# Recurrent heads: the product of decayed keys moved to VectorE alone, in two parts

## The chip, the cores and the metric

The kernel runs on one core of a Trainium2 chip. The metric is device time in microseconds, from the first to the last instruction of one launch with what little lies around it; the median of several runs is taken. Smaller is better.

## The reference: what is computed

One decoder layer on 1024 tokens of width 1024. After an RMS norm, one wide projection feeds two groups of heads: four differential softmax heads and four gated linear attention ("recurrent") heads. Their outputs are normalised, concatenated, projected back and added to the input; a SwiGLU feed-forward block follows. The change lies in the recurrent heads, whose core within a chunk is

```
b = jnp.cumsum(gi, axis=-2)                      # gi: log forget gates, <= 0
diff = b[:, :, :, None, :] - b[:, :, None, :, :]
decay = jnp.exp(jnp.where(causal, diff, -jnp.inf))
A = jnp.einsum('bhtk,bhsk,bhtsk->bhts', qi, ki, decay)
o_intra = jnp.einsum('bhts,bhsv->bhtv', A, vi)
```

The decay differs for each pair of tokens and each key channel, so A is not one plain matrix product.

## The kernel before

**Tiling and stages.** The wide projection runs in eight blocks of columns, each over eight tiles of 128 tokens, as three TensorE products of split float32 operands (function `mm3`, lines 259 to 261). The heads' own work is cut into tasks that a planner (`Order`) places between the steps of the projection by estimated costs and due times, so TensorE always has projection products (`pp`) between those of the heads. Tile then sets the order of the instructions on each engine with its own model, so instructions of different tasks interleave, and it gives each engine's queue its waits. Later come the output projection and the feed-forward block, from about 430 us on; they are not touched.

**The recurrent heads.** They are worked in pairs (class `GlaPair`), and each pair in two halves of 512 tokens. So there are four stretches of this work, starting near 143, 189, 315 and 361 us. In each half there are four windows i = 0 to 3 of 128 tokens. For a window, `factors` (line 618) builds two tiles of seven levels each: X (decayed keys, 128 partitions by 7 x 128) and Q (decayed queries, the same size). A level lv splits the window into blocks of 2^lv tokens and takes the decay of each token against the last token of its neighbouring block:

- differences of the cumulated gates into X: lines 632 and 633, levels 0 to 2 by POOL (GpSimd), levels 3 to 6 by DVE (VectorE);
- one exponential over all of X by ACT (line 634);
- seven products by DVE, one for each level, that write Q from one half of X and the queries (line 638);
- the product of X with the keys kT in place (line 643), levels 0 and 1 by POOL, levels 2 to 6 by DVE. A level of X may be overwritten only after its Q has been read from it.

Then `intra` (line 647) makes the seven products of Q and X on TensorE (line 656), four levels into one PSUM bank and three into another, and DVE copies the masked parts into the tile `at` (line 661, seven instructions). `outputs` (line 665) multiplies `at` with the values (line 673, tile `pgo`). X and Q have two buffers each, so the differences for window i + 2 wait until the products of window i have read X. The banks for the products and for `pgo` come from one ring of two (tag `ms`), so line 673 of window 0 needs a bank from which the four copies of line 661 of window 1 have read.

Of the kernel before, what the change touches and what calls it, by code (L numbers as in the profile page):

```python
# [18 lines left out]
P = 128  # L19
# [9 lines left out]
NLEV = 7  # L29
# [19 lines left out]
def _block_cols(kind, i):  # L49
    if kind == "D":  # L50
        c = [(128 * i, 128), (512 + 128 * i, 128), (1024 + 128 * i, 128)]
        if i == 0:
            c.append((3072, 16))
        return c
    if kind == "A":
        return [(1536 + 128 * i, 128), (1792 + 128 * i, 128), (2048 + 256 * i, 128)]
    return [(2048 + 256 * i + 128, 128), (2560 + 256 * i, 256)]


BLOCK_COLS = [_block_cols(*b) for b in BLOCKS]  # L60
NIN = len(BLOCKS)

OUT_COLS = [(0, 384), (384, 384), (768, 256)]
BLOCK_N = [sum(n for _, n in c) for c in BLOCK_COLS] + [n for _, n in OUT_COLS]
# [94 lines left out]
def decoder_layer(ctx: ExitStack, tc, xt, vecs, lams, w_proj, w_up, w_gu, w_dn, out):  # L159
    nc = tc.nc  # L160
# [92 lines left out]
    def split_scaled(src, gain, hi, lo):  # L253

        nc.scalar.activation(hi, src, AF.Copy, scale=gain)  # L255
        nc.vector.scalar_tensor_tensor(lo, src, gain, hi.bitcast(F32), ALU.mult, ALU.subtract)  # L256
# [44 lines left out]
    def split_unit(b, d, raw):  # L301
# [3 lines left out]
        l = wp.tile([P, n], F32R, name=f"wl{b}_{d}", tag="wl", bufs=9)  # L305
        if b < NIN:
            split_scaled(raw, vec[:, 8 + d : 9 + d], h, l)
# [215 lines left out]
    class GlaPair:  # L523
# [94 lines left out]
        def factors(self, hf, i):  # L618

            p = self.p  # L620


            X = gp.tile([P, NLEV, P], F32, name=f"X{p}_{hf}_{i}", tag="X", bufs=2)
            Q = gp.tile([P, NLEV, 2, 64], F32, name=f"Q{p}_{hf}_{i}", tag="Q", bufs=2)
            o = slice(P * i, P * i + P)
            v4 = lambda a, c: a.rearrange("p (n h c) -> p n h c", h=2, c=c)
            for lv in range(NLEV):
                c = 1 << lv
                xv, bv = v4(X[:, lv, :], c), v4(self.bT[:, o], c)
                ref = bv[:, :, 0, c - 1 : c].to_broadcast([P, 64 // c, c])  # L630
                eng = nc.gpsimd if lv < 3 else nc.vector
                eng.tensor_sub(xv[:, :, 0, :], ref, bv[:, :, 0, :])
                eng.tensor_sub(xv[:, :, 1, :], bv[:, :, 1, :], ref)
            nc.scalar.activation(X, X, AF.Exp)
            for lv in range(NLEV):
                c = 1 << lv
                xv = v4(X[:, lv, :], c)
                nc.vector.tensor_mul(
                    Q[:, lv].rearrange("p g (n c) -> p g n c", c=c),
                    xv[:, :, 1, :].unsqueeze(1).to_broadcast([P, 2, 64 // c, c]),  # L640
                    self.qT[:, :, o].rearrange("p g (n h c) -> p g n h c", h=2, c=c)[:, :, :, 1, :])
            for eng, lvs in ((nc.gpsimd, slice(0, 2)), (nc.vector, slice(2, NLEV))):
                eng.tensor_mul(X[:, lvs], X[:, lvs],  # L643
                               self.kT[:, o].unsqueeze(1).to_broadcast([P, lvs.stop - lvs.start, P]))
            self.XQ[i] = (X, Q)

        def intra(self, hf, i):

            p, (X, Q) = self.p, self.XQ.pop(i)
            at = gp.tile([P, 2, P], F32, name=f"at{p}_{hf}_{i}", tag="at", bufs=3)  # L650
            for hh in range(2):
                nc.scalar.mul(at[:, hh, :], ident8, self.dg[:, 2 * i + hh : 2 * i + hh + 1])
            for lvs in ((0, 1, 2, 3), (4, 5, 6)):
                pa = psum.tile([P, 4, 2, 64], F32, name=f"pa{p}_{hf}_{i}_{lvs[0]}", tag="ms")
                for k, lv in enumerate(lvs):
                    nc.tensor.matmul(pa[:, k], X[:, lv, :], Q[:, lv], start=True, stop=True)  # L656
                for k, lv in enumerate(lvs):
                    c = 1 << lv
                    ov = at.rearrange("p g (n h c) -> p g n h c", h=2, c=c)[:, :, :, 1, :]
                    mv = masks[:, lv, :].rearrange("p (n c) -> p n c", c=c).bitcast(I32)  # L660
                    nc.vector.copy_predicated(ov, mv.unsqueeze(1).to_broadcast([P, 2, 64 // c, c]),
                                              pa[:, k].rearrange("p g (n c) -> p g n c", c=c))
            self.at[hf, i] = at
# [207 lines left out]
    def open_gla():  # L871
        nonlocal gp, gqT, states
        xctx.close()
        gp = gctx.enter_context(pool("gp"))
        states = [gp.tile([P, 256], F32, name=f"S{k}") for k in range(2)]

        gqT = gp.tile([P, 2, 512], F32, name="gqT")
        for S in states + [gqT]:
            nc.gpsimd.memset(S, 0.0)

    for b, (kind, i) in enumerate(BLOCKS):
        obj = heads[i] if kind == "D" else pairs[i]
        evac = obj.evac if kind == "D" else (obj.evac_b if kind == "B" else obj.evac_a)
        for t in range(NT):
# [8 lines left out]
            if b == 0 and t == NT - 1:  # L893
                open_gla()
            if b == NIN - 1 and t % 4 == 3:
                if t == 7:
# [77 lines left out]
    for k, (o, n) in enumerate(OUT_COLS):  # L974
        b = NIN + k
        left = list(range(ND)) if k + 1 < len(OUT_COLS) else []
        for hf in range(2):
# [9 lines left out]
            for cc in range(n // P):  # L987
                c, w = o // P + cc, slice(P * cc, P * cc + P)
# [5 lines left out]
                h = hs[hf][c]  # L994
# [142 lines left out]
    for pr in range(NJ // 2):  # L1137
# [3 lines left out]
        X = [psum.tile([P, 512], F32, name=f"X{pr}_{m}", tag=("mm", "ms")[pr % 2]) for m in range(2)]  # L1141
# [292 lines left out]
```

## Time and profile before

| what | value |
|---|---|
| median of 3 runs | 1241.39 us (1240.34 to 1243.83) |
| the profiled execution, whole | 1245.05 us |
| its span, first to last instruction | 1243.3 us |
| TensorE (PE) busy | 1203.3 us, 97% of the span |
| VectorE (DVE) busy | 878.2 us, 71% |
| ScalarE (ACT) busy | 574.5 us, 46% |
| GpSimd (POOL) busy | 279.9 us, 23% |
| mean granted TensorE clock | 0.993 |

PE is busy nearly throughout, so time can come only from its few stops and from the stretches at a lower granted clock. The busy shares are averages over stages with different limits: what matters is which engine ends last in front of each stop.

### The profile page before, as it was taken

Reading aid. Unit: us, or ns where it says so; the run is one execution under the profiler, and the core shown is the slowest. Engines: PE = TensorE matmul, PEld = TensorE weight load, DVE = VectorE, ACT = ScalarE, POOL = GpSimd, SP = SyncE. Lnnn points to the kernel's source line nnn. Section 1 sums busy time; section 2 is a strip of 40 time slices with the busy share of each in tenths; the row PEclk is TensorE's granted clock in tenths of the full one; section 3 lists DMA queues with packets and bytes.
Section 4 is the critical chain, followed back from the end, with each engine's and each line's share of the span. In section 5 each row is a group of like instructions: output and inputs, shape, how many; then the busy total and the mean of one; then the engine's idle time right before and its main releaser. Section 6 shows DMA issues by size and latency. Waiting matters only on the chain.

```text
span 1243.3 us, 17114 instructions
## 1 busy us (share of the span) xinstructions
PE 1203.3 (97%) x6068; PEld 1012.7 (81%) x6068; DVE 878.2 (71%) x1804; ACT 574.5 (46%) x1171; POOL 279.9 (23%) x282
## 2 busy tenths in 40 slices
PE   7899998999889999999989999999999999999998
PEld 6789888889878978788768888888888888888787
DVE  6864489854888777546997666866677656677885
ACT  5656354555543676534643333333333335444432
POOL 4700314000431000000053434534354330000000
PEclk9999999999999999999999999999999999999999
DMA  6101010102100633221023231322223277743351
GB/s 212 39 28 44 17 52 18 52 26 60 39 31 19 175 96 119 85 93 67 2 102 136 85 114 73 127 94 102 100 87 127 84 254 295 264 153 94 94 178 69
DMA packets 57656, 121.41 MB, mean 98 GB/s; under 512 B 5969, under 2 KB 25570, under 8 KB 53346
## 3 DMA queue, kind: packets, MB, share of 16 engines
q1 hardware_dynamic: 57570, 120.31, 28.5%
q8 instruction: 48, 0.79, 0.3%
q14 instruction: 38, 0.31, 0.1%
HBM read 88.04 MB, written 32.24 MB: 97 GB/s over the span
## 4 chain that ended last, share of the span: by engine, by line
PE 84%; DVE 8%; ACT 3%; DMA 2%; POOL 1%; issue 1%; SPq 0%; DVEq 0%; ACTq 0%; POOLq 0%
PE X L261 6%; PE X L259 6%; PE X L260 6%; PE pp L259 6%; PE pp L261 5%; PE pp L260 5%; PE Z L261 3%; PE Z L260 3%; PE Z L259 3%; PE s L417 3%; PE po L461 3%; PE V L259 2%; PE V L260 2%; PE V L261 2%; PE po L259 2%; PE po L261 2%
## 5 line engine op out<-in xcount | busy, mean ns | idle before, releaser
L259 PE MATMUL pp<-wh,nh 128*128 128x384 f32 (+1 forms) x512 | 186.6, 365 | 9.0 <-ACT wh L255 5.8
L261 PE MATMUL pp<-wh,nl 128*128 128x384 f32 (+1 forms) x512 | 178.1, 348 | 0.0
L260 PE MATMUL pp<-wl,nh 128*128 128x384 f32 (+1 forms) x512 | 178.0, 348 | 0.0
L259 PEld LDWEIGHTS pp<-wh,nh 128*128 128x128 f32 x512 | 99.0, 193 | 19.4 <-ACT wh L255 6.4
L261 PEld LDWEIGHTS pp<-wh,nl 128*128 128x128 f32 x512 | 98.4, 192 | 2.2 <-issue 2.0
L260 PEld LDWEIGHTS pp<-wl,nh 128*128 128x128 f32 x512 | 98.7, 193 | 1.7 <-DVE wl L256 0.8
L1174 POOL TENSOR_TENSOR ac<-ac,gt 128x512 f32<-128x512 f32 x30 | 46.4, 1547 | 161.5 <-DVE ac L1159 153.5
L1080 POOL TENSOR_TENSOR S1f<-fr 128x512 f32<-128x512 f32 x20 | 27.0, 1351 | 246.6 <-DVE ndist L951 238.4
L1171 ACT ACTIVATE gt<-gt 128x512 f32<-128x512 f32 x40 | 25.3, 633 | 112.3 <-DVE gt L1170 59.5
L430 ACT ACTIVATE e<-e,nm 128x128 f32<-128x128 f32 (+7 forms) x64 | 49.3, 771 | 32.9 <-DVE nm L422 32.8
L259 PE MATMUL po<-mh,wh 128*128 128x512 f32 x128 | 51.2, 401 | 0.0
L261 PE MATMUL po<-mh,wl 128*128 128x512 f32 x128 | 50.6, 395 | 0.0
L260 PE MATMUL po<-ml,wh 128*128 128x512 f32 x128 | 50.4, 394 | 0.0
L256 DVE SCALAR_TENSOR_TENSOR wl<-wr,vec,wh 128x384 fp32r<-128x384 f32 (+1 forms) x64 | 40.5, 659 | 9.5 <-ACT wh L255 9.4
L1080 POOL TENSOR_TENSOR S4f<-fr,S2f 128x512 f32<-128x512 f32 x20 | 33.7, 1687 | 53.8 <-DVE ucl L251 51.7
L251 DVE TENSOR_TENSOR ufl<-S3f,ufh 128x512 fp32r<-128x512 f32 x22 | 15.2, 690 | 39.0 <-ACT ufh L250 39.0
L1172 DVE TENSOR_TENSOR gt<-gt,ndist 128x512 f32<-128x512 f32 x40 | 31.6, 790 | 15.8 <-ACT gt L1171 14.0
L461 PE MATMUL po<-v,wT 128*128 128x128 f32 x288 | 39.9, 283 | 2.0 <-ACT wT L451 2.0
L557 POOL TENSOR_TENSOR go<-go,gs 128x1024 f32<-128x1024 f32 x4 | 10.2, 2539 | 140.1 <-ACT gs L556 140.1
L422 DVE CUSTOM_DVE_ANT_0 e<-s,ndist 128x512 f32<-128x512 f32 (+3 forms) x64 | 36.7, 586 | 7.0 <-PE s L417 6.2
L255 ACT ACTIVATE wh<-wr,vec 128x384 fp32r<-128x384 f32 (+1 forms) x64 | 37.5, 615 | 8.8 <-DMA wr<-in_w_proj 7.0
L656 PE MATMUL pa<-Q,X 128*128 128x128 f32 x224 | 32.3, 291 | 9.3 <-POOL X L643 9.2
(555 smaller groups left out, 3535.8 us busy)
## 6 DMA issues: line engine op xcount, KB each, us to landing
fr<-in_w_gu SPq DMA_DIRECT2D x22, 1024.0 KB, 4.9
A<-act SPq DMA_DIRECT2D x77, 256.0 KB, 3.1
wr<-in_w_proj SPq DMA_DIRECT2D x72, 192.0 KB, 2.4
act<-ac SPq DMA_DIRECT2D x11, 1024.0 KB, 3.9
B<-in_w_dn SPq DMA_DIRECT2D x44, 256.0 KB, 5.4
act<-sm SPq DMA_DIRECT2D x11, 768.0 KB, 4.9
h<-in_xt SPq DMA_DIRECT2D x16, 256.0 KB, 5.1
hd<-h SPq DMA_DIRECT2D x16, 256.0 KB, 2.0
```

What stands on the lines that cost most here:

```text
L255: nc.scalar.activation(hi, src, AF.Copy, scale=gain)
L256: nc.vector.scalar_tensor_tensor(lo, src, gain, hi.bitcast(F32), ALU.mult, ALU.subtract)
L259: nc.tensor.matmul(ps, ah, bh, start=first, stop=False, **k)
L260: nc.tensor.matmul(ps, ah, bl, start=False, stop=False, **k)
L261: nc.tensor.matmul(ps, al, bh, start=False, stop=last, **k)
L417: nc.tensor.matmul(ps[m][:, :n], self.qk["q", hq][a][r, P * iq : P * iq + P], self.qk["k", ch][b][r, :n], start=(j == 0), stop=(j == 2))
L422: nc.vector.tensor_tensor_reduce(e[m][:, 512 * ch : 512 * ch + n], ps[m][:, :n], ndist[:, o : o + n], scale=-slope, scalar=nm[:, m, 0:1] i ...
L430: nc.scalar.activation(e[m][:, :cols], e[m][:, :cols], AF.Exp, bias=nm[:, m, nch - 1 : nch], scale=-1.0, accum_out=l[:, m : m + 1])
L461: nc.tensor.matmul(po[:, 0:P], self.wT[i, g][:, P * k : P * k + P], self.v[g][:, k, :], start=(kb == 0), stop=(kb == i))
L656: nc.tensor.matmul(pa[:, k], X[:, lv, :], Q[:, lv], start=True, stop=True)
L1080: (eng.tensor_sub if op == "-" else eng.tensor_add)(r, a, b)
L1174: nc.gpsimd.tensor_mul(quarter(q), quarter(q), g)
```

## The change

The Q products and the key products are done in two parts that follow the two PSUM banks: levels 0 to 3, then levels 4 to 6. In each part DVE makes the Q products of its levels and then one key product over all its levels. POOL no longer takes part in the key product; it keeps the differences of levels 0 to 2. `intra` uses the same table of levels and is otherwise unchanged.

```
+LEVELS = ((0, 1, 2, 3), (4, 5, 6))
...
-            for lv in range(NLEV):
-                c = 1 << lv
-                xv = v4(X[:, lv, :], c)
-                nc.vector.tensor_mul(
-                    Q[:, lv].rearrange("p g (n c) -> p g n c", c=c),
-                    xv[:, :, 1, :].unsqueeze(1).to_broadcast([P, 2, 64 // c, c]),
-                    self.qT[:, :, o].rearrange("p g (n h c) -> p g n h c", h=2, c=c)[:, :, :, 1, :])
-            for eng, lvs in ((nc.gpsimd, slice(0, 2)), (nc.vector, slice(2, NLEV))):
-                eng.tensor_mul(X[:, lvs], X[:, lvs],
-                               self.kT[:, o].unsqueeze(1).to_broadcast([P, lvs.stop - lvs.start, P]))
+            for lvs in LEVELS:
+                for lv in lvs:
+                    c = 1 << lv
+                    xv = v4(X[:, lv, :], c)
+                    nc.vector.tensor_mul(
+                        Q[:, lv].rearrange("p g (n c) -> p g n c", c=c),
+                        xv[:, :, 1, :].unsqueeze(1).to_broadcast([P, 2, 64 // c, c]),
+                        self.qT[:, :, o].rearrange("p g (n h c) -> p g n h c", h=2, c=c)[:, :, :, 1, :])
+                r = slice(lvs[0], lvs[-1] + 1)
+                nc.vector.tensor_mul(X[:, r], X[:, r], self.kT[:, o].unsqueeze(1).to_broadcast([P, len(lvs), P]))
```

## Rows read from the trace of the kernel before

**Rows 1.** The page: busy time, share and instructions of each engine.

```profile
PE 1203.3 (97%) x6068; PEld 1012.7 (81%) x6068; DVE 878.2 (71%) x1804; ACT 574.5 (46%) x1171; POOL 279.9 (23%) x282
```

**Rows 2.** Who waited for whom, PE, 140 to 410 us: total, times, longest.

```profile
PE pa L656 <- POOL X L643: 9.2, 4, 2.8
PE pp L259 <- DVE gv L544: 2.1, 4, 0.6
PE pgo L673 <- DVE at L661: 2.0, 2, 1.0
PE pgo L673 <- DVE X L633: 2.0, 2, 1.0
```

**Rows 3.** Timeline of PE, first and second stretch: start, length, [idle before <- releaser].

```profile
153.36 1.83 PE L656 MATMUL pa<-Q,X 128*128 128x128 f32 x14 [1.78 <-POOL X L643]
...
164.58 0.68 PE L673 MATMUL pgo<-gv,at 128*128 128x128 f32 x4 [1.01 <-DVE X L633]
...
199.46 2.24 PE L656 MATMUL pa<-Q,X 128*128 128x128 f32 x14 [2.82 <-POOL X L643]
...
212.82 0.68 PE L673 MATMUL pgo<-gv,at 128*128 128x128 f32 x4 [1.03 <-DVE at L661]
```

**Rows 4.** Instructions of line 643: count, ns min/median/max, first and last start.

```profile
L643 POOL TENSOR_TENSOR X<-X,gkT x16: 770/1302/3600, 149.7 to 388.9; 128x256 f32<-128x256 f32 x16
L643 DVE TENSOR_TENSOR X<-X,gkT x16: 808/834/1104, 150.7 to 390.0; 128x640 f32<-128x640 f32 x16
```

**Rows 5.** Timeline of POOL, first stretch.

```profile
149.71 4.86 POOL L643 TENSOR_TENSOR X<-X,gkT 128x256 f32<-128x256 f32 x2 [1.70 <-DVE Q L638]
```

**Rows 6.** Timeline of DVE, first stretch (149 to 165 us).

```profile
149.08 1.69 DVE L638 TENSOR_TENSOR Q<-X,gqT 128x128 f32<-128x128 f32 x8
150.70 0.81 DVE L643 TENSOR_TENSOR X<-X,gkT 128x640 f32<-128x640 f32 x1
151.43 1.29 DVE L638 TENSOR_TENSOR Q<-X,gqT 128x128 f32<-128x128 f32 x6
...
152.91 1.08 DVE L643 TENSOR_TENSOR X<-X,gkT 128x640 f32<-128x640 f32 x1
154.56 0.44 DVE L661 COPY_PREDICATED at<-masks,pa 128x128 f32<-128x128 int32 x1 [0.57 <-PE pa L656]
155.29 0.23 DVE L632 TENSOR_TENSOR X<-bT 128x64 f32<-128x64 f32 x1 [0.30 <-PE pa L656]
...
164.16 0.28 DVE L661 COPY_PREDICATED at<-masks,pa 128x128 f32<-128x128 int32 x1
```

**Rows 7.** Timeline of DVE, second stretch.

```profile
195.19 1.69 DVE L638 TENSOR_TENSOR Q<-X,gqT 128x128 f32<-128x128 f32 x8
...
207.30 0.45 DVE L661 COPY_PREDICATED at<-masks,pa 128x128 f32<-128x128 int32 x1 [1.37 <-PE pa L656]
...
209.41 0.23 DVE L632 TENSOR_TENSOR X<-bT 128x64 f32<-128x64 f32 x1 [1.18 <-PE pa L656]
...
211.13 1.14 DVE L638 TENSOR_TENSOR Q<-X,gqT 128x128 f32<-128x128 f32 x2
```

**Rows 8.** Busy time of all engines by stretch, with granted clock (PEclk) and DMA.

```profile
core 0: us, PE busy (x) PEld busy (x) DVE busy (x) ACT busy (x) POOL busy (x), PEclk, DMA share, GB/s
143.00:168.00 25.00, 21.52 (x139) 20.15 (x138) 23.59 (x85) 11.04 (x20) 13.90 (x27) 1.00 0.12 38
188.00:213.00 25.00, 21.12 (x128) 19.99 (x128) 22.11 (x76) 9.36 (x16) 14.18 (x27) 0.93 0.06 22
```

**Rows 9.** PE alone: stretch, length, busy (instructions), granted clock, DMA share, GB/s.

```profile
153.36:156.42 3.06, 3.06 (x22) 1.00 0.01 3
199.46:204.06 4.60, 4.60 (x22) 0.64 0.00 0
...
443.07:446.49 3.42, 3.42 (x16) 0.50 0.42 116
```

**Rows 10.** Timeline of PE near 443 us.

```profile
442.98 1.38 PE L461 MATMUL po<-v,wT 128*128 128x128 f32 x5 [2.00 <-ACT wT L451]
```

More of the change, by code (lines that the diff above doesn't have):

```diff
@@ L652, in intra @@
                 nc.scalar.mul(at[:, hh, :], ident8, self.dg[:, 2 * i + hh : 2 * i + hh + 1])
-            for lvs in ((0, 1, 2, 3), (4, 5, 6)):
+            for lvs in LEVELS:
                 pa = psum.tile([P, 4, 2, 64], F32, name=f"pa{p}_{hf}_{i}_{lvs[0]}", tag="ms")
```

## The prediction

> **What bounds the kernel now.** I read the page first: PE is busy for 97% of the span, DVE for 71%, POOL for 23% [rows 1]. So only PE's stops can be won, and with them time at a lower clock. Next the waits of PE between 140 and 410 us, where the recurrent heads run: it stopped four times, 9.2 us in all, with the products of line 656 waiting for POOL's part of line 643; four times, about 1.0 us each, at line 673 for DVE; and four times, 2.1 us in all, for line 544 on DVE [rows 2]. The timeline shows one long stop in each stretch, at its first window: 1.78 us in the first, 2.82 in the second [rows 3]. The third repeats the first and the fourth the second: (9.2 - 1.78 - 2.82) / 2 is 2.3, the mean of such a pair.
>
> Why POOL is late: its piece of line 643 takes 770 ns at best and 3600 at worst [rows 4]. In the first stretch it begins at 149.71 and two pieces hold it for 4.86 us [rows 5], while DVE runs Q products and its own key product without a gap [rows 6]. POOL's op is slow because it runs beside DVE's.
>
> The trace also prices the long stop's second effect. [...] So each long stop costs 1.5 us more, twice: 3.1 us. Stops and clock together, 9.2 + 3.1 = 12.3 us, are the most that the change can win here.
>
> Last, what else is tight. DVE is busy for 23.59 of 25 us in the first stretch and 22.11 of 25 in the second [rows 8]. That is nearer its limit than the 71% suggests.
>
> **Part by part.** *Removed: 16 POOL pieces.* Behind them on POOL stand only the differences of later windows, which wait for a free buffer of X anyway. What they take from DVE goes too. A DVE key product takes 0.81 us alone and 1.08 beside POOL's [rows 6], a relief of 0.27 for window 1 of each stretch. The two Q products from 211.13 take 1.14 us [rows 7] where one costs 0.20 (eight in 1.62, from 149.08 to 150.70 [rows 6]); POOL's key piece began beside them, and I put 0.5 of the excess down to it, once in each stretch. The late windows of the second and fourth have up to 1.10 [rows 4].
>
> [...]
>
> *Added: key products on DVE.* 640 columns occupy DVE from 150.70 to 151.43, 0.73 us, and 128 columns 0.20 [rows 6], so 1.04 ns a column. 512 columns then cost 0.73 - 0.13 = 0.60 and 384 cost 0.47: 1.07 for 0.73, or 0.33 more a window, 1.3 a stretch, 5.3 in all. Bounds from the same rows: 0.27 (256 columns with no cost for the second instruction) and 0.41 (two Q products' worth).
>
> *The first wait of line 656.* First stretch: DVE begins its Q products at 149.08 [rows 6]; four take 0.81, the first key part 0.60, and about 0.1 passes to PE (from the end of two Q products, 149.57, to POOL's start at 149.71 [rows 5]). X is ready at 150.6. PE arrived at 153.36 - 1.78 = 151.58 [rows 3], so it doesn't stop. The second part is ready by 150.5 + 0.61 + 0.47 + 0.1 = 151.7, and the first bank keeps PE busy until about 152.6. Second stretch: start at 195.19 [rows 7], X at 196.7, PE at 196.64: a stop of 0.1 remains. If the order puts window 1's work ahead, one Q or two, 0.2 to 0.4, come back. So nearly all of the 9.2 us goes at this place, and with it the 3.1 of the clock.
>
> *What is late next.* Line 673. It waits for a bank, and so for the fourth copy (line 661) of window 1, at 164.16, whose end comes just before 164.58 [rows 3, 6]. From 149.08 to there DVE idles only 0.57 and 0.30 us, both waiting for the late products [rows 6]. So PE's earlier arrival doesn't make line 673 as much earlier; DVE's work does. First stretch: idle won 0.87, relief 0.27, windows 0 and 1 cost 0.66, and ahead of that copy stand 512 columns of window 2 instead of 640, 0.13: 0.87 + 0.27 - 0.66 + 0.13 = 0.6 us earlier. Second: idle won 1.37 + 1.18 [rows 7] = 2.55, relief 0.27 + 0.5, cost 0.66, and the new first key part may now come ahead of the copy (0 or 0.60; middle 0.3): 2.4 us. Twice each: 6.0 us.
>
> Whether that carries to the end: behind line 673 DVE's further cost, 0.33 a window, meets the rest of the relief and no stop above 0.6 us [rows 2]. The other way, the stop at line 673 would grow: 1.01 + 1.78 - 0.6 = 2.2 us in the first stretch, 1.03 + 2.72 + 1.54 - 2.4 = 2.9 in the second. A stop of 2.00 us at 442.98 [rows 10] was followed by a clock of 0.50 [rows 9]; one of 1.78 was not. How many of the four would be is open: 0 to 4 of 1.5 us. Against it, the order on PE is made anew with DVE's larger load known to it; projection products can fill the place ahead of line 673, and then more than 6.0 is won. I take these two as cancelling.
>
> **The sum.** 6.0 us off the profiled execution: 1245.05 (span 1243.3 and 1.75 around it) becomes 1239.1. That execution lies 3.7 above the median of 1241.39, so the median becomes 1235.4.
>
> **Rivals.** *Full gain.* The stops vanish and projection products fill the place ahead of line 673, so its stops stay near 1 us: 12.3 less 0.2 to 0.4 for the second and fourth stretch, about 11.8: 1229.6. For it: the work of PE there is only reordered. Against: DVE's 94% [rows 8].
>
> *The wait moves.* The order stays, the stops at line 673 grow to 2.2 and 2.9 us and all four bring the lower clock: 6.0 - 4 x 1.5 = 0: 1241.4. For it: DVE's unbroken run in the first stretch [rows 6]. That the split doesn't do what it says belongs here: if both parts come back to back in DVE's queue, the first bank waits 1.1 us more, which costs the second and fourth stretch about 1 us each, and the time stays within 0.3%.
>
> *DVE becomes the bound: slower.* Place: DVE's queue ahead of line 673. It decides once none of the idle time there is won, because the copies stand behind window 2's two key parts. Each stretch then pays three windows, 3 x 0.33 = 1.0 us, and the first and third pay a lower clock that they didn't have, 2 x 1.5: 4.0 + 3.0 = 7.0 less 2 for relief, 5: 1246.4. Against: DVE does idle 2.55 us in the second stretch [rows 7].
> [...]
>
> **How the numbers follow.** Chances: forecast 0.43, full gain 0.20, the wait moves 0.25, DVE bound 0.12. About 0.3%, 3.7 us, is what a measurement of this kernel can tell from no change. The forecast's spread, 3 to 9 us, reaches a little over that line: 0.37 of it is faster. Faster 0.20 + 0.37 = 0.57; same 0.25 + 0.06 = 0.31; slower 0.12. The range reaches from the full gain, 1229, to a little past no change, 1244, leaving out most of the slower rival.
>
> **What would show it.** Line 643 only on DVE, 32 instructions of 0.6 to 0.7 us (512 columns) and 0.5 to 0.6 (384). No wait of line 656 above 0.4 us; if one stays, the first step is wrong. Line 673: stops of 1 us and clock 1.00 behind them speak for full gain, stops over 2 us with a clock near 0.5 for the moved wait. DVE's idle time between 188 and 213 us should fall from 25 - 22.11 = 2.9 us [rows 8] to under 1. The Q product beside POOL's key piece should be back at 0.20 us. The prediction is wrong if the new order puts other stops elsewhere: at line 544, or behind 410 us, where nothing in the code changes.

## The result and the profile after

| what | before | after |
|---|---|---|
| median | 1240.61 us (5 runs, 1236.34 to 1243.83) | 1228.66 us (5 runs, 1228.18 to 1230.50) |
| ratio, 95% interval | | 0.9896 (0.9878 to 0.9914) |
| profiled execution, whole | 1245.05 us | 1228.34 us |
| its span | 1243.3 us | 1226.6 us |

The kernel became faster by 12 us, twice the 6.0 us forecast and a third of a microsecond outside the range. The two profiled executions lie 16.7 us apart, more than the medians. The part above 12 is not put down to the change: in the execution of before, two stretches at half clock fell behind the heads' part, 0.50 from 443.07 us [rows 9] and 0.51 from 637.6 to 641.0; after, the wait at the first place came out at 1.87 us for 2.00 [rows 10], and the clock stayed at 1.00 at both.

The page after, busy time and instructions by engine; it answers to [rows 1].

```profile
PE 1195.2 (97%) x6068; PEld 1005.9 (82%) x6068; DVE 875.8 (71%) x1820; ACT 573.1 (47%) x1171; POOL 259.5 (21%) x266
```

POOL lost its 16 pieces and 20 us. DVE has 16 instructions more and still 2.4 us less busy time.

Who waited for whom, PE, in the heads' part of the changed kernel; it answers to [rows 2].

```profile
PE pp L261 <- DVE gv L546: 3.1, 4, 0.9
PE pa L659 <- DVE X L635: 1.4, 2, 0.7
PE pa L659 <- DVE X L647: 0.8, 2, 0.4
PE pa L659 <- DVE d_y L247: 0.6, 2, 0.3
PE pa L659 <- DVE S L693: 0.4, 2, 0.2
```

The four long stops, 9.2 us, are 0.8 us now (line 647 is the old 643). The four stops at the old line 673, 4.0 us, are gone altogether, which was not forecast. New are stops in front of the products of windows 1 and 2, 2.4 us in all (lines 635, 247 and 693), and those in front of projection products grew by 1.0 us, from 2.1 to 3.1. In sum PE's stops fell by 9.0 us on these rows.

The timeline of PE after; it answers to [rows 3]. Lines 659 and 676 are the old 656 and 673.

```profile
150.70 1.72 PE L659 MATMUL pa<-Q,X 128*128 128x128 f32 x14
155.37 1.13 PE L659 MATMUL pa<-Q,X 128*128 128x128 f32 x8 [0.66 <-DVE X L635]
...
162.10 0.68 PE L676 MATMUL pgo<-gv,at 128*128 128x128 f32 x4
...
194.54 1.92 PE L659 MATMUL pa<-Q,X 128*128 128x128 f32 x14 [0.38 <-DVE X L647]
...
205.12 0.68 PE L676 MATMUL pgo<-gv,at 128*128 128x128 f32 x4
```

The timeline of DVE after, second stretch, around window 1's copies (line 664, the old 661); it answers to [rows 7].

```profile
203.21 0.43 DVE L664 COPY_PREDICATED at<-masks,pa 128x128 f32<-128x128 int32 x1
203.44 0.32 DVE L365 TENSOR_SCALAR v<-pp,rsx 128x128 f32<-128x128 f32 x1
203.68 0.45 DVE L664 COPY_PREDICATED at<-masks,pa 128x128 f32<-128x128 int32 x1
...
204.34 0.30 DVE L664 COPY_PREDICATED at<-masks,pa 128x128 f32<-128x128 int32 x1
...
204.67 0.30 DVE L664 COPY_PREDICATED at<-masks,pa 128x128 f32<-128x128 int32 x1
205.05 1.42 DVE L642 TENSOR_TENSOR Q<-X,gqT 128x128 f32<-128x128 f32 x5
```

All four copies that free the bank for line 676 now stand ahead of window 2's Q products. Before, the fourth stood behind them. In the first stretch it still does: there the fourth copy starts at 161.67 us, behind window 2's Q products and first key product, and PE's projection products reach just as far, so that line 676 starts at 162.10 without a stop.

Busy time by stretch after (PE, PEld, DVE, ACT, POOL, granted clock, DMA); it answers to [rows 8].

```profile
143.00:168.00 25.00, 23.69 (x153) 22.42 (x153) 24.88 (x95) 11.37 (x21) 9.36 (x24) 1.00 0.16 49
188.00:213.00 25.00, 24.28 (x156) 22.20 (x155) 24.83 (x96) 9.92 (x18) 7.93 (x22) 1.00 0.06 22
```

DVE is busy for all but 0.1 and 0.2 of 25 us, and PE does 2.2 and 3.2 us more in the same 25 us. The clock is 1.00 in both.

### The profile page after: what moved, and what is told of

Same layout as the page of the kernel before. It is cut to its first block, busy times and chain, and to the rows that moved or that the text cites. A ratio compares the mean times of both kernels' runs of the same rounds, so it can differ in the third digit from the quotient of the medians.

```text
span 1226.6 us, 17086 instructions
## 1 busy us (share of the span) xinstructions
PE 1195.2 (97%) x6068; PEld 1005.9 (82%) x6068; DVE 875.8 (71%) x1820; ACT 573.1 (47%) x1171; POOL 259.5 (21%) x266
## 4 chain that ended last, share of the span: by engine, by line
PE 79%; DVE 14%; ACT 3%; issue 2%; DMA 2%; SPq 0%; DVEq 0%; ACTq 0%
PE X L263 6%; PE X L261 6%; PE X L262 6%; PE pp L261 5%; PE pp L263 5%; PE pp L262 4%; PE Z L263 3%; PE Z L262 3%; PE Z L261 3%; PE s L419 3%; PE po L463 2%; PE po L261 2%; PE po L263 2%; PE po L262 2%; PE V L263 2%; PE V L261 2%
## 5 line engine op out<-in xcount | busy, mean ns | idle before, releaser
L634 POOL TENSOR_TENSOR X<-bT 128x64 f32<-128x64 f32 x48 | 20.3, 423 | 118.9 <-ACT bT L603 82.9
L559 POOL TENSOR_TENSOR go<-go,gs 128x1024 f32<-128x1024 f32 x4 | 10.2, 2542 | 146.9 <-ACT gs L558 146.9
```

## Experiments

All times are medians; a ratio, with its 95% interval, is against the kernel before on the same chip, whose median was 1241.6 to 1242.1 us in these runs. The ratio on record isn't exactly the quotient of the two medians; differences in us below are those of the medians.

### The engine alone, without the split

```
-            for eng, lvs in ((nc.gpsimd, slice(0, 2)), (nc.vector, slice(2, NLEV))):
+            for eng, lvs in ((nc.vector, slice(0, NLEV)),):
```

> The kernel before with one edit: all seven levels of the key product by VectorE, in one instruction after the seven Q products; no split by banks. Theory A (what counts is that GpSimd leaves the key product): the first wait of line 656 shrinks from 1.78 us to about 0 in the first and third stretch and from 2.82 to about 1.1 in the second and fourth (seven Q products 1.42 + 1.0 for 896 columns from 195.19, PE there at 196.64), the clock stays up: about 1231 us. Theory B (the split by banks carries the gain): the wait stays near its old length, 1237 to 1241 us.

Measured: 1229.61 us, ratio 0.9897 (0.9877 to 0.9916). The first waits of line 656:

```profile
PE pa L656 <- DVE X L643: 2.8, 4, 1.1
```

Theory A holds. The waits came out near what was worked out (0.34 us for about 0, and 1.03 for about 1.1), and the time is level with the changed kernel's. The split by banks takes 2 us off these waits, but nothing off the time that can be measured.

### The split alone, GpSimd keeping its levels

```
+                for eng, r in ((nc.gpsimd, slice(0, 2)), (nc.vector, slice(2, 4))) if lvs[0] == 0 else ((nc.vector, slice(4, 7)),):
```

> The two parts by banks as in the changed kernel, but GpSimd keeps levels 0 and 1 of the first part. Theory A: GpSimd's first piece is still slow beside VectorE's Q products, the four long waits of line 656 stay: within 2 us of the kernel before, 1239 to 1243. Theory B (the split carries the gain): 1229 to 1233 us.

Measured: 1244.75 us, ratio 1.0026 (1.0015 to 1.0037).

```profile
PE pa L659 <- POOL X L647: 10.8, 4, 3.2
```

Theory B falls: without the change of engine the split costs 0.3%, and the long stops grow from 9.2 to 10.8 us. The stops stayed, as theory A has it; the time lies 1.8 us above its range.

### Window 0 alone, and windows 1 to 3 alone

```
+            new = i == 0        # the other kernel: i > 0
+            for lvs in LEVELS if new else (tuple(range(NLEV)),):
...
+                for eng, r in ((nc.vector, slice(lvs[0], lvs[-1] + 1)),) if new else (
+                        (nc.gpsimd, slice(0, 2)), (nc.vector, slice(2, NLEV))):
```

> The new form in window 0 of each half alone; windows 1 to 3 as before, with GpSimd's piece. Theory A (the four long stops and the lower clock behind two of them are the gain): nearly all of it, 1229 to 1231 us. Theory C (what GpSimd's other twelve pieces take from VectorE counts too): 3 to 4 us short of the changed kernel, about 1232.5 us.

Measured: 1233.04 us, ratio 0.9930 (0.9916 to 0.9943): 8.6 us.

> The complement of the run on window 0: the new form in windows 1 to 3 alone, GpSimd's piece kept in window 0. The four long stops at the first wait of line 656 stay (9.2 us) and so does the lower clock behind two of them; what GpSimd's other pieces take from VectorE is gone. Theory C (window 0 alone gained 8.6 of 12 us, the rest is this): 1237 to 1239 us. If the parts don't add (VectorE's relief is worth something only once the stops are gone): 1240 to 1242.

Measured: 1242.32 us, ratio 1.0000 (0.9986 to 1.0013): nothing.

```profile
152.71 1.83 PE L661 MATMUL pa<-Q,X 128*128 128x128 f32 x14 [2.39 <-POOL X L649]
...
163.27 0.68 PE L678 MATMUL pgo<-gv,at 128*128 128x128 f32 x4 [0.16 <-DVE at L666]
...
199.02 2.84 PE L661 MATMUL pa<-Q,X 128*128 128x128 f32 x14 [3.43 <-POOL X L649]
```

Window 0 carries most of the gain, as theory A has it, but the time is theory C's: the other twelve pieces are worth 4.4 us once window 0's are gone, and nothing while they are there. With window 0's pieces in place, the stop at line 673 goes (0.16 us here) and the stop ahead of it grows by 0.6 us each time. The parts don't add; theory C's sum for the second run was wrong by that.

### The order of the copies held as before

```
...
+                    if i == 1 and lv >= 2 + hf:
+                        tc.add_manual_dep(cp.ins, self.last_q[2].ins.name, mybir.DependencyInfo(
+                            mybir.DependencyClass.NoSync, mybir.DependencyReason.DATA), reason="held")
```

This is an order on DVE's queue, not a wait. With it, window 1's copies stand around window 2's Q products as in the kernel before.

> The changed kernel, with the order on VectorE at one place held as in the kernel before: of window 1's copies (line 661) only two (first half) or three (second half) go ahead of window 2's Q products. Theory D (the prediction fell short because these copies moved ahead of window 2 when the order was made anew): line 673 starts 0.7 us later in the first and third stretch and 2.7 in the second and fourth, PE stops there, 4 to 7 us slower than the changed kernel, 1233 to 1236 us, more if the clock falls. Theory E (TensorE has enough other work in any order, the place of the copies is worth nothing): 1228 to 1230 us.

Measured: 1230.71 us, ratio 0.9909 (0.9893 to 0.9925).

```profile
162.83 0.68 PE L680 MATMUL pgo<-gv,at 128*128 128x128 f32 x4 [0.33 <-DVE at L665]
...
208.57 0.68 PE L680 MATMUL pgo<-gv,at 128*128 128x128 f32 x4 [0.47 <-DVE at L665]
```

Line 673 did start later against the stretch's first matrix product (line 596): 23.3 us after it in the second stretch instead of 20.4. But PE hardly stopped there. In the second stretch 46 projection products stood between the first product of line 656 and line 673, against 33 in the changed kernel and 37 before: PE's order had been made anew around the later copies. Theory D is mostly wrong, E mostly right, its range missed by 0.7 us: with PE's order free, the copies' place costs 2.0 us by the medians, and the intervals of the two kernels overlap.

### Both orders held as before

The same, and the projection products that stood behind line 673 before are queued behind it on PE as well.

```
...
+                    if at <= (b, t, d, n) < (at[0], at[1] + 2, 0, 0):
+                        tc.add_manual_dep(mm.ins, first_pgo[key], mybir.DependencyInfo(
+                            mybir.DependencyClass.NoSync, mybir.DependencyReason.DATA), reason="held")
```

> As the kernel with the copies held, and the projection products that stood behind line 673 of window 0 in the kernel before are held behind it here too. So this is the order that the prediction worked with. Theory F (the gain behind line 673 hangs on projection products being moved ahead of it): TensorE stops at line 673 for 1.2 to 2 us in the first and third stretch and 2 to 2.9 in the second and fourth, with the clock falling behind some of these; 4 to 8 us slower than with the copies alone held, 1234 to 1239 us, near the 1235.4 predicted. Theory G (what isn't done ahead of line 673 is made up later): within 2 us of it, 1229 to 1232.

Measured: 1235.11 us, ratio 0.9936 (0.9918 to 0.9955).

```profile
161.44 0.68 PE L691 MATMUL pgo<-gv,at 128*128 128x128 f32 x4 [0.43 <-DVE at L676]
...
207.16 0.57 PE L691 MATMUL pgo<-gv,at 128*128 128x128 f32 x3 [1.78 <-DVE at L676]
...
375.52 0.68 PE L691 MATMUL pgo<-gv,at 128*128 128x128 f32 x4 [1.77 <-DVE at L676]
```

PE alone, by stretch: length, busy, granted clock, DMA share, GB/s.

```profile
207.20:210.50 3.30, 3.30 (x24) 1.00 0.00 0
...
375.52:379.00 3.48, 3.48 (x15) 0.61 0.00 0
```

Theory F, by its time. This run puts the order that the prediction worked with on the chip, but for the transposes named below, and its time is near the prediction's: 1235.1 us for 1235.4, 6.7 us less than before where 6.0 was forecast (5.6 to 10.2 by the ratio's interval). The stops at line 673 are 1.78 us in the second and fourth stretch (2.9 forecast) and 0.43 in the first and third (2.2 forecast, but there seven transposes of the next half slipped in ahead). Behind one of the two long stops, 1.77 us, the clock fell to a mean of 0.61; behind the other, 1.78 us, it stayed at 1.00.

### GpSimd's differences: one level more, one level less

```
-                eng = nc.gpsimd if lv < 3 else nc.vector
+                eng = nc.gpsimd if lv < 4 else nc.vector   # the other kernel: lv < 2
```

> The changed kernel, with the differences of level 3 moved from VectorE to GpSimd (levels 0 to 3 there). VectorE, busy for 24.9 of 25 us in the first stretch, loses 32 instructions of 0.135 us, 4.3 us. If VectorE is the bound now: 1225 to 1228 us. If GpSimd's differences (0.29 us each alone, more beside VectorE) then end last in front of the exponential: 1229 to 1234.

Measured: 1230.45 us, ratio 0.9905 (0.9883 to 0.9928).

> The other way: the differences of level 2 moved from GpSimd to VectorE, 32 instructions of 0.135 us more there. If VectorE is the bound: 1230 to 1233 us. If the Q products are held up more by GpSimd's differences (0.30 us beside them for 0.20 alone) than by that: 1226 to 1228.

Measured: 1234.43 us, ratio 0.9935 (0.9917 to 0.9953).

```profile
PE pa L659 <- DVE X L647: 3.7, 4, 1.0
PE pgo L676 <- DVE at L664: 3.4, 2, 1.7
```

4.3 us more on DVE cost about 5 us (the rows are of this second kernel: stops at line 676 are back). 4.3 us less bought nothing, and if anything cost a little. So more load on DVE cost time here and less won none, and three levels on GpSimd stay the best of the three. The first run's time lies in the range of its second theory; that GpSimd's differences ended last in front of the exponential there isn't shown. The second run's time lies 1.4 us above its nearer theory.

### A pause for GpSimd, with no work moved

In the kernel before, window 0 of each half gets one DVE instruction more: a sum over 64 columns of Q's level 3, which nothing uses. The orders of Q products, key products and copies are those of before.

```
+                if i == 0 and lv == 3:
+                    scr = small.tile([P, 1], F32, name=f"scr{p}_{hf}_{i}", tag="scr")
+                    nc.vector.reduce_sum(scr, Q[:, 3, 0, :], axis=AX.X)
```

> The kernel before, with one instruction added: in window 0 of each half VectorE sums 64 columns of Q's level 3 right behind that level's product (four instructions in all; the sum isn't used). In every trace so far GpSimd's slow piece of line 643 ended 0.65 to 0.68 us after the start of the first VectorE instruction that isn't a product of two SBUF tiles (line 544, 363 or 690). Theory H (the piece stands still until VectorE's run of such products is broken, whatever breaks it): with the sum at about 150.1 the piece ends near 150.8 instead of 153.3, and takes about 1.1 us instead of 3.6; the wait of line 656 shrinks to VectorE's own chain, 0.4 us or less in the first and third stretch and about 1 in the second and fourth, the clock stays up: 1231 to 1235 us, with no work moved. Theory I (the piece is slow because VectorE is busy at all, or by its size): the wait and the time stay, 1240 to 1243 us.

Measured: 1235.88 us, ratio 0.9953 (0.9934 to 0.9973). The piece of POOL and the sum in the first stretch (two timelines), and PE's waits:

```profile
146.00 1.06 POOL L646 TENSOR_TENSOR X<-X,gkT 128x256 f32<-128x256 f32 x1 [1.71 <-DVE Q L638]
```

```profile
146.37 0.22 DVE L644 TENSOR_REDUCE scr<-Q 128x1 f32<-128x64 f32 x1
```

```profile
PE pgo L676 <- DVE at L664: 2.0, 2, 1.0
PE pgo L676 <- DVE X L633: 1.9, 2, 0.9
PE pa L659 <- DVE X L633: 1.6, 2, 1.0
PE pa L659 <- DVE X L646: 1.2, 2, 0.6
...
PE pa L659 <- POOL X L646: 0.6, 2, 0.3
```

Theory H. The piece took 1.06 us instead of 3.60; it ended 0.69 us after the sum's start. The sum started where the next product would have, 0.20 us after the one before it, so DVE had no gap there. PE's wait for the piece fell from 9.2 to 0.6 us, and the stops at line 673 (676 here) stayed at 1 us as before, since the order was kept. Some of what was won came back as stops for DVE ahead of line 659, 2.8 us in the two rows shown. Four instructions of 0.2 us won some 6 us. The interval is wide (3 to 8 us); the size is near the held order's 6.7.

> The same sum in all sixteen windows. Theory H: as with window 0 alone, within 2 us of it; in the later windows the piece already got its turn. Theory I: 1241 to 1244 us.

Measured: 1237.92 us, ratio 0.9959 (0.9946 to 0.9973): the same within the intervals. The later windows get nothing from it.

### Two parts in window 0, one part in the others

```
+            for lvs in LEVELS if i == 0 else (tuple(range(NLEV)),):
```

> All key products on VectorE, in two parts in window 0 alone and in one instruction in windows 1 to 3: the changed kernel with 12 instructions fewer. If the split is worth what it saves of the first wait (0.4 us instead of 1.1 in the second and fourth stretch) and costs 0.06 us an instruction: 1227 to 1229 us, level with the changed kernel or a little faster. If the order made anew decides more than that: anywhere from 1227 to 1232.

Measured: 1229.56 us, ratio 0.9901 (0.9885 to 0.9917). Level with the changed kernel, as was the kernel without any split: neither shows a gain from the split. No kernel's median was below the changed one's.

## Why the prediction was wrong

**The reading of the stops held.** The long stops were GpSimd's pieces, 9.2 us, with a lower clock behind two of them, 0.64 [rows 3, 9] and 0.69 (the row below). They went nearly whole: to 0 and 0.38 us, where 0 and 0.1 were worked out, with 0.2 to 0.4 more if window 1's Q products came ahead, as one did. The price of the clock, 1.5 us a stop and 3.1 in all, was a difference of two rows: 22 products took 4.60 us at a mean granted clock of 0.64 and 3.06 at 1.00 [rows 9]. It was a little high: the fourth stretch was taken to be like the second, and there 24 products took 4.62 us.

```profile
371.94:376.56 4.62, 4.62 (x24) 0.69 0.00 0
```

At the full clock 24 would have taken 3.4 by estimate (22 took 3.06 [rows 9], and each further product of 384 columns 0.17 from start to start), so some 1.2 us was lost there, not 1.5. The runs on the engine alone and on the split alone show that it is GpSimd's part that did it.

**The price of the key products held.** Measured from start to start, 512 columns take 0.60 us and 384 take 0.47, as worked out from [rows 6]. The relief was there too: a Q product beside GpSimd's piece had been held for 0.5 us [rows 7], and it was larger than forecast; the longest Q product took 0.83 us before and 0.41 after. In the heads' part the key products' busy time rose by only 4.9 us (14.7 to 19.6) and that of the Q products fell by 1.9 (28.3 to 26.4). DVE's fall of 2.4 us in all isn't a measure of it: 2.1 us of it lie in a line of code that runs only behind 430 us, where nothing was changed.

**What is late next: the sum held, for the order of before.** Line 673 was forecast to come 0.6 us earlier in the first and third stretch and 2.4 in the second and fourth. With both orders held it came 0.9 and 2.4 us earlier in the first and second (161.44 - 139.12 = 22.3 us after the stretch's first product of line 596 for 23.3, and 23.3 for 25.7), and the time was 1235.1 us.

**The step that failed** is "I take these two as cancelling". On one side stood stops at line 673 that grow to 2.2 and 2.9 us, on the other projection products that fill that place because the order is made anew. They don't cancel: in the changed kernel the stops are 0, not 2.2 and 2.9 us, and the reordering alone comes true. It came on DVE as well, where the sum kept the order of before. In the first stretch 41 projection products stood between the first product of line 656 and line 673, 39 before. In the second it was 33 for 37, and there the copies moved ahead on DVE let line 673 start sooner after line 596 (20.4 us, and 23.3 with the copies held). The three kernels with DVE's new load form a ladder: both orders held 1235.1 us, the copies' order held and PE's order free 1230.7, both free 1228.7. The intervals of the two ends lie just apart and that of the middle overlaps both: that the two reorderings count together is shown, and how the 6.4 us between the ends divide (4.4 and 2.0 by the medians) isn't. The reorderings, which the edit nowhere spells out, are thus about half of the 12 us.

The rival "full gain" comes nearest, with 1229.6, and got a chance of only 0.20. That it came so near is in part luck. Its sum left line 673 at 1 us and had no new stops; the rows after show 4.0 us won at line 673, 2.4 lost in new stops and 1.0 in larger ones, and the 0.6 that remains is small. The prediction had named such stops elsewhere as a sign of being wrong, at line 544 (now 546) among others; there the longest grew from 0.6 to 0.9 us. What spoke against the full gain, DVE's 94% [rows 8], turned out no hindrance: DVE went to 99.5% in the first stretch and PE did more in it, not less.

There may have been a sign in the rows of before: the stop at line 673 was about 1.0 us in all four stretches [rows 2], however long the earlier stop. That could be the trace of an order made to reach this place at a set distance, so that it would be made so again for a new load. This is a reading; no run tests it.

**The size of the stops in the held order** was also off: 2.2 and 2.9 forecast, 0.43 and 1.78 measured. In the first stretch transposes of the next half took part of the place; why the other is 1.1 us short isn't shown. That the time still came out at the forecast's is therefore partly luck. The clock fell behind one of the two longest (0.61) and not behind the other (1.00); 0 to 4 falls were left open.

**The rivals.** "The wait moves" needed the held order, and even there the time fell by 6.7 us. Of "DVE becomes the bound" something appears when more is put on DVE: with the differences of level 2 as well, stops at line 673 are back (two, 3.4 us) and the time is 1234.4 us. But it didn't decide here: DVE was busy for 94% of the first stretch [rows 8], and taking work back from GpSimd made the kernel 1.0% faster.

**What stays open.** Why one level more on GpSimd brought nothing although it takes 4.3 us from DVE: the orders differ there too, and no run held them. How the 6.4 us of the two reorderings divide between PE and DVE. And the 4.7 us by which the two profiled executions differ beyond the medians are placed only roughly, in the two further stretches at half clock.

## What to carry to other kernels

When PE waits for a GpSimd elementwise instruction that takes several times its best time (3.60 us for 0.77 here), look at what DVE runs beside it: here an unbroken run of products of two SBUF tiles held it up. One DVE instruction of 0.21 us of another kind among them brought PE's wait for it from 9.2 us to 0.6; moving the work to DVE left 0.8 us in front of the same products. When a planner orders the queues, a change of one engine's load can move the neighbours on other engines too. A forecast with the old order then prices the edit alone (6.0 us forecast and 6.7 measured of the 12 here), and an order held by edges is the run that shows which part was the edit and which the planner.

## What the runs showed of the hardware

GpSimd's slow piece wasn't slowed evenly; it ended as if it had stood still until DVE's run was broken. In four kernels (before, window 0 alone, the split alone, windows 1 to 3 alone) the pieces that took 1.4 us or more ended 0.65 to 0.68 us after the start of the first DVE instruction of another kind, whether they had begun 0.8 or 3.5 us ahead of it. ("Of another kind" is one that isn't a product of two SBUF tiles; besides a column of scalars, each of these reads at most one tile from SBUF.) Here are the longest (windows 1 to 3 alone: POOL, then DVE):

```profile
148.46 4.20 POOL L649 TENSOR_TENSOR X<-X,gkT 128x256 f32<-128x256 f32 x1 [1.70 <-DVE Q L643]
```

```profile
151.59 0.48 DVE L643 TENSOR_TENSOR Q<-X,gqT 128x128 f32<-128x128 f32 x2
152.00 0.34 DVE L546 TENSOR_SCALAR gv<-pp,rsx 128x128 f32<-128x128 f32 x1
152.26 0.81 DVE L649 TENSOR_TENSOR X<-X,gkT 128x384 f32<-128x384 f32 x1
```

The piece lasts 4.20 us, from 148.46 to 152.66; line 546, which reads PSUM, starts at 152.00. DVE's own 384-column product from 152.26, with the last 0.40 us of the piece beside it, takes 0.81 us; the one at 150.57 in the changed kernel, with no GpSimd instruction beside it, takes 0.54. So DVE was held up too, by 0.27 us. GpSimd's piece was held up over a whole run of DVE instructions, not over one: in the kernel before, eleven products began on DVE between the piece's start at 149.71 us and line 544 at 152.64, and the piece took 3.60 us where the shortest took 0.77. With the pause of 0.22 us in that run it took 1.06 us. Four pieces of the kernel before began inside such a run and don't fit: those at 169.25, 211.35, 341.74 and 383.58 took 0.77 to 0.86 us and held up a Q product by 0.5 us instead (up to 0.83 us, the shortest 0.27), with no other instruction of DVE beside them. In the kernel with the pause in window 0 alone, the first stretch's piece of window 1 took 1.46 us and ended 0.68 after the start of line 544 (148.70 and 149.48). What decides whether a piece gets its turn at once stays open.

With both orders held, a mean clock of 0.61 followed a stop of 1.77 us (375.52 to 379.00), and 1.00 one of 1.78 in the same execution (207.20 to 210.50), so a stop's length alone doesn't tell it.
